# Chunk 0 of a hybrid decoder block's MLP as seven block products, with the block sums of chunks 0 to 2 formed by transfers

## The chip, the cores and the metric

The kernel runs on one core of one Trainium2 chip. The metric is the device time of one execution in microseconds (us); a kernel's time is the median of several executions. TensorE (PE; PEld is its weight load), VectorE (DVE), ScalarE (ACT), GpSimd (POOL) and SyncE (SP) each run their own instructions in order and wait for one another through semaphores.

## The reference

One layer of a causal decoder on 256 tokens of width 1024, all in float32: a convolution branch and a sparse attention branch from one input projection, a cross attention over 256 memory tokens, and a squared-ReLU MLP. The change lies in the MLP:

```python
hf = _rmsnorm(h, norm_ffn_g[l]) @ w_ff1[l]             # 1024 -> 4096
h = h + jnp.square(jax.nn.relu(hf)) @ w_ff2[l]         # 4096 -> 1024
...
return _rmsnorm(h, norm_final_g)
```

## The kernel before

*Numbers.* Matrix products are made in float32r from operands split in two: `hi` is the rounded value (a Copy on ScalarE), `lo` the rest (a subtraction on VectorE). A product a @ b is three matmuls, a_hi b_hi + a_hi b_lo + a_lo b_hi (`mm3`). With activations held as hi and lo side by side, an f1 tile can be "wide": eight matmuls of 512 columns and eight of 256 in place of 24 narrow ones of 256. A wide tile leaves two halves that must be merged (a Copy on ScalarE, line 444, and an add on VectorE); a narrow one goes straight into the Relu (line 1208).

*The weight stream.* All weights come in 1 MB chunks through transfers issued on SP's queue (`fetch`, line 178), into three rotating `raws` buffers, and for some chunks into `t8` buffers. `high_jobs` lists what is to be split next; `split_high` issues one ScalarE copy (line 295 in `high`, line 273 in `seven`) if a slot is free (six `highs`/`lows`, less those held), and `split_low` issues the VectorE subtraction of the copy before. `split_ahead` calls both, and a step of TensorE's work calls it once or so. A chunk's buffer is handed back by `release`, which issues the next load. The order of all engines' instructions is thus written out by the program; nothing is moved by a scheduler.

*The chains.* Work that follows a product (activations, norms, the 16 small transfers that turn `h_t` into `h_rm`, line 1200) is written as generators. Each `tick` advances every running generator by one `yield`, and so places its next instructions into the engines' queues at that point.

*The MLP.* f1 and f2 are cut into 16 chunks of 256 hidden features. `first` makes chunk c + 2's f1 tiles (two of 128 features), and `half_of` adds chunk c's part to the output, half before and half after the second f1 tile. Tokens are two row blocks of 128, and f2's chunk is a 2 x 2 block matrix (128 x 512 each). Chunks 1 to 13 (`SEVEN`) use a seven-product scheme: four stages `left`, `last`, `outer` and `inner` with 2, 1, 2 and 2 block products, which need sums of f2's blocks (`sums`) and differences of the activations' blocks (`t[:, 4:8]` in `activation`). VectorE forms the four sums of a chunk with one add of 128x1024 and two of 128x512 (`outer` and `inner` in `seven`). ScalarE's copies of the sums read them directly. Chunk 0 is instead made with eight products (`half_of`, `c not in SEVEN`), and its activation goes by halves (`by_halves`); chunk 2's f1 tiles, made beside chunk 0, are wide, those of the later chunks narrow (`wide` in the loop). f1 of chunks 0 and 1 comes before the loop, through `form_b_late` and `form_b`.

*Banks.* The seven partial sums stay open in PSUM over all chunks: "2", "3", "4", "5" in the four `ps_acc` banks, "7" in one of the two `ps_mm` banks, "1" and "6" in the two `ps_aux`. f1's tiles of the loop use what is left of `ps_mm`.

*POOL.* GpSimd issues 25 adding transfers for the convolution (line 628, `accum_op=ALU.add`, 256 KB each) up to 172 us, a few small operations, and one memset of `table` near the end of the program (line 1423). Line 81 is the helper through which all TensorE and VectorE instructions are recorded.

Of the kernel before, what the change touches and what calls it, by code (L numbers as in the profile page):

```python
# [8 lines left out]
F32 = mybir.dt.float32  # L9
# [3 lines left out]
ALU = mybir.AluOpType  # L13
# [3 lines left out]
P = 128  # L17
D = 1024
S = 256
KT = D // P  # L20
# [33 lines left out]
INDEX = {c: n for n, c in enumerate(c for c in STREAM if c[0] != "ki")}  # L54
# [2 lines left out]
HALVES = 6  # L57
EARLY = (3,)
WHOLE = (("conv", 0),)
SEVEN = tuple(range(1, 14))  # L60
JOINED = 14
FIRST = STREAM.index(("f1", 2))
BY_HALVES = ()

# [51 lines left out]
def block_kernel(ctx, tc, x, xt, mem, memt, wst, wki, vecs, convw, gout, out):  # L116
# [15 lines left out]
    def t8(name, dt=F32, shape=(P, KT, S)):  # L132
        return big.tile(list(shape), dt, tag="t8", bufs=12, name=name)
# [16 lines left out]
    def ps_acc(name):  # L150
        return bank("acc", 4, name)
# [12 lines left out]
    prepared, whole, elsewhere = {}, {}, set()  # L164
    order = [c for c, key in enumerate(STREAM) if key[0] != "f1" or key[1] < 3]
    early = set(EARLY)
    raw_of, landed = {}, set()
    high_jobs, low_jobs = [], []

    def fetch(c, raw, parts=1, only=None):  # L170

        key = STREAM[c]
        n = KT * NK if key[0] == "ki" else N_CHUNK
        src = wki if key[0] == "ki" else wst[INDEX[key]]
        for q in range(parts):
            if only in (None, q):
                ns = slice(q * n // parts, (q + 1) * n // parts)
                nc.sync.dma_start(raw[:, ns], src[:, ns])
        raw_of[c] = raw
        landed.update((key, q) for q in ((0, 1) if only is None else (only,)))  # L180
# [61 lines left out]
    def seven(key, c):  # L242

        def b():
            return raw_of[c].rearrange("p (k h n) -> p k h n", k=2, h=2)

        def flat():
            return raw_of[c].rearrange("p (j n) -> p j n", j=4)

        sums = []  # L250

        def outer():
            sums.append(t8(f"sums{c}", F32, (P, 4, 512)))
            dve.tensor_tensor(out=sums[0][:, 0:2, :], in0=flat()[:, 0:4:3, :],
                              in1=flat()[:, 1:2, :].to_broadcast([P, 2, 512]), op=ALU.add)

        def inner(j):
            t = sums[0]
            dve.tensor_tensor(out=t[:, j, :], in0=t[:, j - 1, :], in1=flat()[:, 2 * j - 4, :], op=ALU.add)
            if j == 3:  # L260
                release(key, c, 1, True)

        def stage(name, src_of, n, steps=()):
            def high():
                src = src_of()
                if steps:
                    both = t8(f"{name}{c}", F32R, (P, 2, 2, 512))
                    hi, lo = both[:, 0], both[:, 1]
                else:
                    hi = highs.tile([P, N_CHUNK // 2], F32R, tag="hi", name=f"hi{c}{name}")  # L270
                    lo = lows.tile([P, N_CHUNK // 2], F32R, tag="lo", name=f"lo{c}{name}")
                    hi, lo = (w[:, : n * 512].rearrange("p (j n) -> p j n", j=n) for w in (hi, lo))
                act(hi, src, AF.Copy)  # L273

                def low():
                    dve.tensor_tensor(out=lo, in0=src, in1=hi.bitcast(F32), op=ALU.subtract)
                    prepared[(*key, name)] = (hi, lo)

                low_jobs.append(low)

            return Stage((*key, name), high, steps, not steps, (key, 0))

        return [stage("left", lambda: b()[:, :, 0, :], 2), stage("last", lambda: flat()[:, 3:4, :], 1),
                stage("outer", lambda: sums[0][:, 0:2, :], 2, (outer,)),
                stage("inner", lambda: sums[0][:, 2:4, :], 2, (lambda: inner(2), lambda: inner(3)))]

# [35 lines left out]
    def weights(kind, i, half, kt):  # L322

        key = (kind, i, half)
        while key not in prepared:
            split_high()
            split_low()
        nused[0] += key not in elsewhere
        return [w if kt is None else w.rearrange("p (k n) -> p k n", k=kt) for w in prepared.pop(key)]
# [18 lines left out]
    def split_ahead():  # L348
        split_low()
        split_high()  # L350

    def tick():
        for c in list(chains):
            if next(c, "end") == "end":
                chains.remove(c)
        while (len(fill) > 1 or (fill and (len(done) > 5 or nused[0] < 5))) and dve.total < pe.total - 1000:
            fill_one()
        dve.total = max(dve.total, pe.total - 2000)
        add_some()
# [30 lines left out]
    def tile_b(ps, w, x2, kts=range(KT), wide=False, late=False):  # L390


        ps = ps[: w[0].shape[2]]
        for kt in kts:
            wh, wl = w[0][:, kt, :], w[1][:, kt, :]
            if not wide:
                mm_b(ps[:, :S], wh, wl, x2, kt, kt == 0, kt == KT - 1)
            elif kt == 0:
                pe.matmul(ps, wh, x2.both(kt), start=True, stop=False)
                if late:  # L400
                    pe.matmul(ps[:, S:], wl, x2.high(kt), start=False, stop=False)
            elif not late:
                pe.matmul(ps, wh, x2.both(kt), start=False, stop=False)
            else:
                pe.matmul(ps[:, S:], wl, x2.high(kt), start=False, stop=False)
                pe.matmul(ps, wh, x2.both(kt), start=False, stop=kt == KT - 1)
        for kt in kts if wide and not late else ():
            pe.matmul(ps[:, S:], w[1][:, kt, :], x2.high(kt), start=False, stop=kt == KT - 1)
# [5 lines left out]
    def form_b(kind, i, x2, after, ps_of=ps_mm):  # L414

        for ct in range(2):
            w = weights(kind, i, ct, KT)
            split_ahead()
            ps = ps_of(f"ps_{kind}{i}{ct}")
            wide = is_wide(kind, 2 * i + ct)  # L420
            tile_b(ps, w, x2, wide=wide)
            after(2 * i + ct, ps if wide else ps[:, :S])
            tick()
# [753 lines left out]
    for hf in range(2):  # L1177
        nc.sync.dma_start(g_out[hf], gout[hf * 512 : hf * 512 + 512].partition_broadcast(P))
    fetch(STREAM.index(("f1", 3)), t8("raw_f1", F32, (P, N_CHUNK)))
    r2 = []  # L1180

    def ff_scale():
# [31 lines left out]
    def part(c, t, js, sh, sl):  # L1214
        act(sh[:, js, :], t, AF.Copy)
        yield
        dve.tensor_tensor(out=sl[:, js, :], in0=t, in1=sh[:, js, :].bitcast(F32), op=ALU.subtract)

    def by_halves(c, ct, ps, t, sh, sl):
        js = slice(2 * ct, 2 * ct + 2)  # L1220
        yield from relu(ps, t[:, js, :].rearrange("p r n -> p (r n)"))
        act(t[:, js, :], t[:, js, :], AF.Square)
        yield
        yield from part(c, t[:, js, :], js, sh, sl)
        if c == 0 and ct:
            dve.tensor_tensor(out=t[:, 4:6, :], in0=t[:, 1:4:2, :], in1=t[:, 0:4:2, :], op=ALU.subtract)
            yield
            yield from part(c, t[:, 4:6, :], slice(4, 6), sh, sl)

    def activation(c, ct, ps, t, sh, sl):  # L1230
        if c in (0, 15):
            yield from by_halves(c, ct, ps, t, sh, sl)
            return
        yield from relu(ps, t[:, 2 * ct : 2 * ct + 2, :].rearrange("p r n -> p (r n)"))
        if ct == 0:
            return
        act(t[:, 0:4, :], t[:, 0:4, :], AF.Square)
        yield
        js = slice(0, 4)
        if c in SEVEN:  # L1240

            dve.tensor_tensor(out=t[:, 4:6, :], in0=t[:, 0:1, :].to_broadcast([P, 2, P]), in1=t[:, 1:3, :], op=ALU.subtract)
            yield
            dve.tensor_tensor(out=t[:, 6, :], in0=t[:, 1, :], in1=t[:, 5, :], op=ALU.subtract)
            yield
            dve.tensor_tensor(out=t[:, 7, :], in0=t[:, 3, :], in1=t[:, 6, :], op=ALU.subtract)
            yield
            js = slice(1, 8)
        elif c < JOINED:
            dve.tensor_tensor(out=t[:, 4:6, :], in0=t[:, 1:4:2, :], in1=t[:, 0:4:2, :], op=ALU.subtract)  # L1250
            yield
            js = slice(0, 6)
        yield from part(c, t[:, js, :], slice(0, js.stop - js.start), sh, sl)
# [21 lines left out]

    hidden = [Hidden(0), Hidden(1)]
    form_b_late("f1", 0, f2, hidden[0].after, ps_of=ps_acc)
    form_b("f1", 1, f2, hidden[1].after, ps_acc)

    uses = {}  # L1280
    for c in range(JOINED):
# [35 lines left out]
    def first(x, side, wide):  # L1317
        ps = ps_mm(f"ps_f{x.c}{side}")
        w = weights("f1", x.c, side, KT)
        split_ahead()  # L1320
        tile_b(ps, w, f2, wide=wide)
        x.after(side, ps if wide else ps[:, :S])
        tick()
        if wide:
            tick()
# [188 lines left out]
```

## Time and profile before

| | us |
|---|---|
| median of 3 runs (501.36 to 501.70) | 501.44 |
| the profiled execution | 501.41 |
| its span, first to last instruction | 499.6 |
| TensorE busy | 490.8 (98%) |
| VectorE busy | 465.5 (93%) |
| ScalarE busy | 349.0 (70%) |
| GpSimd busy | 30.6 (6%) |

The profiled execution's time lies 0.03 us under the median, so its rows can be set against the runs as they are. Times in rows are us from the span's start. The MLP begins at about 322.6 (the first f1 matmul) and the last f2 matmul ends at 488.3. Line 81 appears for nearly all TensorE and VectorE rows, so these are told apart by the tiles they write and read (`ps_f` for f1, `ps_p` for f2's products, `fs` and `ft` for activations, `sums`, `outer`, `inner` for the seven scheme). Instructions overlap their neighbours by some 0.09 us on VectorE, so the sum of durations is a little over the time taken.

### The profile page before, as it was taken

Reading aid. Unit: us, or ns where it says so; the run is one execution under the profiler, and the core shown is the slowest. Engines: PE = TensorE matmul, PEld = TensorE weight load, DVE = VectorE, ACT = ScalarE, POOL = GpSimd, SP = SyncE. Lnnn points to the kernel's source line nnn. Section 1 sums busy time; section 2 is a strip of 40 time slices with the busy share of each in tenths; the row PEclk is TensorE's granted clock in tenths of the full one; section 3 lists DMA queues with packets and bytes.
Section 4 is the critical chain, followed back from the end, with each engine's and each line's share of the span. In section 5 each row is a group of like instructions: output and inputs, shape, how many; then the busy total and the mean of one; then the engine's idle time right before and its main releaser. Section 6 shows DMA issues by size and latency. Waiting matters only on the chain.

```text
span 499.6 us, 8287 instructions
## 1 busy us (share of the span) xinstructions
PE 490.8 (98%) x3120; PEld 444.3 (89%) x3120; DVE 465.5 (93%) x847; ACT 349.0 (70%) x606; POOL 30.6 (6%) x47
## 2 busy tenths in 40 slices
PE   7999999999999999999999999999999999999995
PEld 6999998888888889888889999988999999999984
DVE  5999899999999789999988997799999999999996
ACT  7657777788756666767846567687777667777752
POOL 2002212221111100000000000000000000000000
PEclk9999999999999999999999999999999999999999
DMA  8959688899887653444655553765666456655412
GB/s 317 378 190 280 174 195 264 238 243 279 240 219 224 180 178 104 152 169 173 249 169 183 220 188 110 269 186 132 195 234 222 171 185 213 234 208 173 131 81 84
DMA packets 28376, 100.35 MB, mean 201 GB/s; under 512 B 10784, under 2 KB 11552, under 8 KB 19376
## 3 DMA queue, kind: packets, MB, share of 16 engines
q1 hardware_dynamic: 24416, 93.03, 54.7%
q0 software_dynamic: 3632, 6.59, 7.4%
q8 instruction: 24, 0.39, 0.3%
q10 hardware_dynamic: 288, 0.20, 0.1%
q14 instruction: 16, 0.13, 0.1%
HBM read 91.16 MB, written 1.05 MB: 185 GB/s over the span
## 4 chain that ended last, share of the span: by engine, by line
PE 92%; DVE 5%; DMA 1%; ACT 1%; issue 1%; POOL 0%; DVEq 0%; SPq 0%; ACTq 0%; POOLq 0%
PE ps_f L81 18%; PE ps_p L81 15%; PE ps_conv L81 10%; PE ps_co L81 5%; PE ps_ao L81 4%; PE ps_ga L81 4%; PE ps_gc L81 4%; PE ps_q L81 4%; PE ps_k L81 4%; PE ps_v L81 4%; PE ps_xo L81 3%; PE ps_qi L81 2%; PE ps_xk L81 2%; PE ps_xv L81 2%; PE ps_xq L81 2%; PE ps_mix L81 1%
## 5 line engine op out<-in xcount | busy, mean ns | idle before, releaser
L81 DVE TENSOR_TENSOR lo<-raw,hi 128x1024 fp32r<-128x1024 f32 x133 | 161.2, 1215 | 3.3 <-ACT hi L295 3.0
L295 ACT ACTIVATE hi<-raw 128x1024 fp32r<-128x1024 f32 x133 | 138.5, 1046 | 0.9 <-DMA raw<-in_wst_dram 0.9
L81 PE MATMUL ps_f<-ff_p,hi 128*128 128x256 f32 (+1 forms) x464 | 89.2, 294 | 0.0
L81 PEld LDWEIGHTS ps_f<-ff_p,hi 128*128 128x128 f32 x464 | 75.3, 191 | 3.7
L81 DVE SCALAR_TENSOR_TENSOR acc<-u,cw,acc 128x234 f32<-128x234 f32 (+29 forms) x190 | 78.1, 463 | 0.3
L81 PE MATMUL ps_f<-ff_p,lo 128*128 128x256 f32 x256 | 67.5, 283 | 0.0
L81 PEld LDWEIGHTS ps_f<-ff_p,lo 128*128 128x128 f32 x256 | 47.2, 191 | 0.4
L81 PE MATMUL ps_conv<-n_p,hi 128*128 128x256 f32 x224 | 41.0, 285 | 0.0
L81 PEld LDWEIGHTS ps_conv<-n_p,hi 128*128 128x128 f32 x224 | 34.9, 192 | 0.8 <-issue 0.7
L81 PE MATMUL ps_conv<-n_p,lo 128*128 128x256 f32 x112 | 31.7, 283 | 0.0
L628 POOL DMA_DIRECT2D acc<-products x25 | 21.7, 867 | 125.6 <-ACT products L627 53.1
L273 ACT ACTIVATE inner<-sums 128x1024 fp32r<-128x1024 f32 x13 | 13.8, 1061 | 20.6 <-DVE sums L81 20.6
L627 ACT ACTIVATE products<-u,cw 128x231 f32<-128x231 f32 (+24 forms) x50 | 21.9, 488 | 0.0
L81 PEld LDWEIGHTS ps_conv<-n_p,lo 128*128 128x128 f32 x112 | 21.5, 192 | 0.0
L1208 ACT ACTIVATE ft<-ps_f 128x256 f32<-128x256 f32 x26 | 9.9, 380 | 14.7 <-PE ps_f L81 14.7
L81 PE MATMUL ps_p<-outer,fs 128*128 128x512 f32 x78 | 20.1, 393 | 0.0
L81 PE MATMUL ps_v<-hi,n_p 128*128 128x512 f32 x64 | 19.9, 389 | 0.0
L81 PE MATMUL ps_p<-inner,fs 128*128 128x512 f32 x78 | 19.8, 389 | 0.0
L81 PE MATMUL ps_co<-u_p,hi 128*128 128x512 f32 (+1 forms) x80 | 19.3, 350 | 0.0
L81 PE MATMUL ps_mix<-mix_p,hi 128*128 128x512 f32 (+1 forms) x80 | 19.2, 349 | 0.0
L81 DVE TENSOR_TENSOR sums<-sums,raw 128x512 f32<-128x512 f32 x26 | 17.8, 684 | 0.0
L81 PEld LDWEIGHTS ps_p<-inner,fs 128*128 128x128 f32 x78 | 14.6, 188 | 3.0
(424 smaller groups left out, 1168.0 us busy)
## 6 DMA issues: line engine op xcount, KB each, us to landing
raw<-in_wst_dram SPq DMA_DIRECT2D x67, 1024.0 KB, 5.5
raw<-in_wst_dram SPq DMA_DIRECT2D x28, 512.0 KB, 4.4
acc<-products POOLq DMA_DIRECT2D x25, 256.0 KB, 6.4
x_rm<-in_x_dram SPq DMA_DIRECT2D x2, 512.0 KB, 4.0
mem_rm<-in_mem_dram SPq DMA_DIRECT2D x1, 1024.0 KB, 9.1
mem_t<-in_memt_dram SPq DMA_DIRECT2D x1, 1024.0 KB, 11.1
h_t<-in_xt_dram SPq DMA_DIRECT2D x1, 1024.0 KB, 6.9
raw_f<-in_wst_dram SPq DMA_DIRECT2D x1, 1024.0 KB, 9.5
```

The lines of the kernel that those rows point to most:

```text
L81: return fn(*args, **kwargs)
L273: act(hi, src, AF.Copy)
L295: act(hi, raw[:, ns], AF.Copy)
L627: act(prod[:, a, s:], u[:, t, : S - s], AF.Copy, scale=cw[:, t, TAPS - 1 - s : TAPS - s])
L628: nc.gpsimd.dma_start(acc[:, ts, :], prod, accum_op=ALU.add)
L1208: act(t, ps, AF.Relu)
```

## The change

Chunk 0 joins `SEVEN`. For chunks 0, 1 and 2 (`ADDED`) the block sums are no longer made by VectorE. Right after the load of f1's chunk 3 is issued, POOL issues for each of them two plain transfers of 512 KB from the weights in HBM into a `sums` tile, then an adding one of 512 KB (its second block, read twice), an adding one within SBUF of 512 KB (`sums[1]`, read twice), and an adding one of 256 KB; chunks 0 and 1 go side by side, chunk 2 after them. Chunk 0's `outer` and `inner` use `highs`/`lows` slots instead of `t8` buffers. In the activations of chunks 0 to 2 two `yield`s between the small subtractions are dropped. f1's tiles of chunk 1 get two ticks ahead of `after` and one behind it, and chunk 2's tiles one more.

```diff
-SEVEN = tuple(range(1, 14))
+SEVEN = tuple(range(14))
 JOINED = 14
+ADDED = (0, 1, 2)
...
         def outer():
+            if added:
+                sums.append(added_sums[key[1]])
+                return
             sums.append(t8(f"sums{c}", F32, (P, 4, 512)))
             dve.tensor_tensor(out=sums[0][:, 0:2, :], ...)
         def inner(j):
             t = sums[0]
-            dve.tensor_tensor(out=t[:, j, :], in0=t[:, j - 1, :], in1=flat()[:, 2 * j - 4, :], op=ALU.add)
+            if not added:
+                dve.tensor_tensor(out=t[:, j, :], in0=t[:, j - 1, :], in1=flat()[:, 2 * j - 4, :], op=ALU.add)
             if j == 3:
                 release(key, c, 1, True)
...
-                if steps:
+                if steps and key[1] > 0:
                     both = t8(f"{name}{c}", F32R, (P, 2, 2, 512))
...
-            return Stage((*key, name), high, steps, not steps, (key, 0))
+            return Stage((*key, name), high, steps, not steps or key[1] == 0, (key, 0))
...
     fetch(STREAM.index(("f1", 3)), t8("raw_f1", F32, (P, N_CHUNK)))
+    for group in ((0, 1), (2,)):
+        for c in group:
+            added_sums[c] = t8(f"sums{c}", F32, (P, 4, 512))
+        blocks = {c: wst[INDEX[("f2", c)]].rearrange("p (j n) -> p j n", j=4) for c in group}
+        for c in group:
+            nc.gpsimd.dma_start(added_sums[c][:, 0:2, :], blocks[c][:, 0:4:3, :])
+            nc.gpsimd.dma_start(added_sums[c][:, 2:4, :], blocks[c][:, 0:4:2, :])
+        for c in group:
+            nc.gpsimd.dma_start(added_sums[c][:, 0:2, :], blocks[c][:, 1:2, :].to_broadcast([P, 2, 512]), accum_op=ALU.add)
+        for c in group:
+            nc.gpsimd.dma_start(added_sums[c][:, 2:4, :], added_sums[c][:, 1:2, :].to_broadcast([P, 2, 512]), accum_op=ALU.add)
+        for c in group:
+            nc.gpsimd.dma_start(added_sums[c][:, 3, :], blocks[c][:, 0, :], accum_op=ALU.add)
...
-        if c == 0 and ct:
-            dve.tensor_tensor(out=t[:, 4:6, :], in0=t[:, 1:4:2, :], in1=t[:, 0:4:2, :], op=ALU.subtract)
-            yield
-            yield from part(c, t[:, 4:6, :], slice(4, 6), sh, sl)
     def activation(c, ct, ps, t, sh, sl):
-        if c in (0, 15):
+        if c == 15:
             yield from by_halves(c, ct, ps, t, sh, sl)
...
             dve.tensor_tensor(out=t[:, 4:6, :], in0=t[:, 0:1, :].to_broadcast([P, 2, P]), in1=t[:, 1:3, :], op=ALU.subtract)
-            yield
+            if c > 2:
+                yield
             dve.tensor_tensor(out=t[:, 6, :], in0=t[:, 1, :], in1=t[:, 5, :], op=ALU.subtract)
-            yield
+            if c > 2:
+                yield
             dve.tensor_tensor(out=t[:, 7, :], in0=t[:, 3, :], in1=t[:, 6, :], op=ALU.subtract)
...
     form_b_late("f1", 0, f2, hidden[0].after, ps_of=ps_acc)
-    form_b("f1", 1, f2, hidden[1].after, ps_acc)
+    for side in range(2):
+        w = weights("f1", 1, side, KT)
+        split_ahead()
+        ps = ps_acc(f"ps_f11{side}")
+        tile_b(ps, w, f2, wide=True)
+        tick()
+        tick()
+        hidden[1].after(side, ps)
+        tick()
...
         tile_b(ps, w, f2, wide=wide)
+        if x.c == 2:
+            tick()
         x.after(side, ps if wide else ps[:, :S])
         tick()
```

`first` is called with `wide = c not in SEVEN and c != 5` for chunk c + 2, so with chunk 0 in `SEVEN` no f1 tile of the loop is wide.

More of the change, by code (lines that the diff above doesn't have):

```diff
@@ L166, in block_kernel @@
     early = set(EARLY)
-    raw_of, landed = {}, set()
+    raw_of, landed, added_sums = {}, set(), {}
     high_jobs, low_jobs = [], []
@@ L248, in flat @@
             return raw_of[c].rearrange("p (j n) -> p j n", j=4)
-        sums = []
+        sums, added = [], key[1] in ADDED
         def outer():
+            if added:
+                sums.append(added_sums[key[1]])
+                return
             sums.append(t8(f"sums{c}", F32, (P, 4, 512)))
```

## The prediction

> **What bounds the kernel now.** I read the engine shares first, then the chain that ended last, then its pieces in order of time around the MLP's first chunks, where the edits lie.
>
> ```profile
> span 499.6 us, 8287 instructions
> PE 490.8 (98%) x3120; PEld 444.3 (89%) x3120; DVE 465.5 (93%) x847; ACT 349.0 (70%) x606; POOL 30.6 (6%) x47
> PE 92%; DVE 5%; DMA 1%; ACT 1%; issue 1%; POOL 0%; DVEq 0%; SPq 0%; ACTq 0%; POOLq 0%
> ```
>
> TensorE carries 92% of the chain, so an edit pays only where it shortens TensorE's own work or closes one of its gaps. The pieces (start, length, what):
>
> ```profile
> 292.19 3.74 PE ps_xq L81 x29
> ...
> 306.54 1.13 PE ps_xs L81 x4
> ...
> 322.64 13.97 PE ps_f L81 x80
> 336.61 0.34 PE ps_ff L81 x4
> 336.95 3.09 PE ps_p L81 x12
> 340.04 2.77 PE ps_f L81 x16
> 342.81 2.75 PE ps_p L81 x12
> 345.56 2.87 PE ps_f L81 x24
> 348.43 2.07 PE ps_p L81 x9
> 350.50 2.87 PE ps_f L81 x24
> 353.37 2.75 PE ps_p L81 x12
> 356.12 2.87 PE ps_f L81 x24
> 358.99 2.07 PE ps_p L81 x9
> 361.06 2.87 PE ps_f L81 x24
> ```
>
> From 322.64 every piece begins where the last one ends: five wide f1 tiles (13.97 / 5 = 2.79 each), the four small matmuls of the row norms, chunk 0 as 24 matmuls (3.09 + 2.75) around a wide tile of chunk 2 (2.77), then chunk 1 with narrow tiles (2.87) and 9 + 12 matmuls (2.07 + 2.75). Twelve matmuls that wait for nothing take 2.75; chunk 0's first twelve take 3.09. The 0.34 between is the one gap, and the waits name it (total, times, longest):
>
> ```profile
> PEld ps_p L81 <- ACT fs L1215: 0.3, 1, 0.3
> PEld ps_p L81 <- DVE fs L81: 0.2, 1, 0.2
> ```
>
> That is chunk 0's activation, finished too late for its first products. VectorE has no reserve in this stage, but ends early enough (third row: columns PE, PEld, DVE, ACT busy, DMA share next to last):
>
> ```profile
> 38.00:172.00 134.00, 134.00 (x841) 120.01 (x840) 129.71 (x285) 98.04 (x183) 25.47 (x29) 1.00 0.83 235
> 297.00:322.00 25.00, 24.90 (x187) 23.80 (x186) 18.48 (x39) 16.91 (x38) 0.35 (x2) 1.00 0.57 200
> 337.00:359.00 22.00, 22.00 (x134) 19.44 (x134) 21.34 (x32) 15.79 (x24) 0.00 (x0) 1.00 0.64 161
> ```
>
> **The change part by part.** *Chunk 0 as seven products.* 24 matmuls become 21, in the 9 + 12 of chunk 1: 2.07 + 2.75 = 4.82 in place of 3.09 + 2.75 = 5.84. Of the 1.02 saved, 0.68 is three matmuls and 0.34 the gap, if it closes. Chunk 0 in SEVEN also makes both f1 tiles of chunk 2 narrow: 2 x (2.87 - 2.77) = +0.20. Sum on TensorE: -0.82.
>
> *Chunk 0's activation and the ticks.* Its chain grows (one Square over both halves, three small subtractions, one copy and one subtraction of 896 columns), so does the gap close? The edit gives the f1 tiles of chunk 1 three ticks each instead of one, and drops two yields, so the chain's steps stand earlier in every queue. I laid the queues out by hand from the rows of before: VectorE frees up at 328.7, then one 1.22 split, three 0.69 and 0.42 adds for the norm's sums, the merge of the second half (0.42), the three subtractions (0.42, 0.28, 0.28), the split of "left" (1.22), a merge, the norm's two scalars, and chunk 0's last subtraction (1.08) come to 336.5, each start being some 0.09 before the end of the one ahead.
>
> ```profile
> L81 DVE TENSOR_TENSOR fs<-ft,fs 128x896 fp32r<-128x896 f32 x13 | 14.1, 1083 | 0.0
> L81 DVE TENSOR_TENSOR ft<-ft 128x128 f32<-128x128 f32 x26 | 7.4, 284 | 0.0
> 338.37 0.42 DVE L81 TENSOR_TENSOR fs<-ft,fs 128x256 fp32r<-128x256 f32 x1
> ```
>
> The first product would be ready to start at 322.64 + 4 x 2.79 + 0.34 + 2.87 = 337.0, so the operand is there 0.5 early, where it ended at 338.8 before. Bounds: nothing to +0.8, the latter if every margin of 0.5 that I find for chunk 0 (also "outer" and the f1 half of chunk 3) is missed by a little. I take zero.
>
> *The norm's four small matmuls* move ahead of chunk 2's first tile, because of the ticks. They need the folded sums, by my layout at 332.5, and TensorE reaches them at 333.8. Cost zero, bound 0.3. The transfers of h_rm, one a tick, also go out some four ticks earlier on SP's queue, 0.63 each, ahead of loads that may so start up to 2.5 late.
>
> *Block sums off VectorE.* Chunks 1 and 2 lose one 128x1024 and two 128x512 adds each.
>
> ```profile
> L81 DVE TENSOR_TENSOR sums<-raw 128x1024 f32<-128x1024 f32 x13 | 15.8, 1218 | 0.0
> L81 DVE TENSOR_TENSOR sums<-sums,raw 128x512 f32<-128x512 f32 x26 | 17.8, 684 | 0.0
> ACT inner L273 <- DVE sums L81: 20.6, 12, 2.7
> ```
>
> That is 1.22 + 2 x 0.68 = 2.59 per chunk, and chunk 0's seven form would otherwise have cost the same. The time is worth nothing by itself, since TensorE does not wait for VectorE after 340; it is what makes room for chunk 0's extra splits (left, last, outer, inner: 1.22 + 0.68 + 1.22 + 1.22 against the two of 1.22 before).
>
> *The transfers on POOL's queue.* Per chunk two plain 512 KB transfers, two adding 512 KB and one adding 256 KB, fifteen in all. POOL is free early, and the one thing queued behind them, the clearing of `table` at 317.44, is read only by the last norm, at the end.
>
> ```profile
> 296.55 0.70 POOL L501 TENSOR_TENSOR rs_cx<-ms_cx,half 128x2 f32<-128x2 f32 x1 [64.48 <-DVE ms_cx L81]
> 317.44 0.10 POOL L1423 MEMSET table<- 128x1 f32 x1 [20.19 <-ACT table L1130]
> L628 POOL DMA_DIRECT2D acc<-products x25: 852/862/908, 38.9 to 172.4; - x25
> DMA to landing us min/median/max: 3.3/6.4/8.9
> q1 hardware_dynamic: 24416, 93.03, 54.7%
> q0 software_dynamic: 3632, 6.59, 7.4%
> ```
>
> The buffers are no hindrance: sums 0 and 1 take those of mix_p, whose last matmul is ahead of the piece at 292.19, and sums 2 that of qx, last read by the piece at 306.54. So the first group starts at 297.3. The price of one adding transfer is in the trace: 25 of 256 KB from POOL's queue (the convolution taps) landed after 3.3 to 8.9 us, median 6.4. For size I use the queues' shares: q0 took 0.074 x 499.6 / 6.59 = 5.6 us per MB of all 16 engines, q1 0.547 x 499.6 / 93.03 = 2.9. So 512 KB adding is 6.4 + 1.5 = 7.9, and 512 KB plain 6.5 (1.5 of transfer in either case). Sums 2 wait for seven landings one behind another, since POOL issues in order and waits for chunk 1's second adds before it comes to the second group: plain 299.0 to 305.5; adds of chunk 1, behind chunk 0's on the same ring (+1.5), to 314.9 and 324.3; issue of the last add; plain to 331.7; adds to 339.6, 347.5 and, 256 KB, 353.9. With every landing at its shortest it is 332, with every one at its longest 371. Sums 0 are whole four landings after 297.3, by some 328, sums 1 by 332.
>
> When are they needed? ScalarE copies inner of chunk 0 at about 339.5 by my layout, of chunk 1 at 348. For chunk 2 the trace shows how late the copy may be:
>
> ```profile
> 359.18 1.06 ACT L273 ACTIVATE inner<-sums 128x1024 fp32r<-128x1024 f32 x1 [2.70 <-DVE sums L81]
> 360.15 0.37 ACT L1208 ACTIVATE ft<-ps_f 128x256 f32<-128x256 f32 x1
> ```
>
> Behind it in ScalarE's order stands the Relu that empties the bank of chunk 4's first f1 tile. The product "7" holds one of the two ps_mm banks, so the next f1 tile (361.06) waits for that Relu, which ended at 360.52: 0.54 to spare. The copy may thus start at 359.18 + 0.54, less the 0.82 that TensorE is ahead: 358.9. My 353.9 leaves 5 us. That is a cover and not a certainty: each us beyond 358.9 is a us of TensorE.
>
> A rule speaks against this. The Trainium skill (SBUF — State Buffer, "SBUF: two separate sides") says that transfers issued from GpSimd starve while VectorE runs in a two-port mode, because their descriptors can't be written. The 25 landings above carry whatever of that there is: VectorE was busy 129.71 of 134.00 us there, at a DMA share of 0.83, as against 18.48 of 25.00 at 0.57 and 21.34 of 22.00 at 0.64 where the new transfers run. So the median may be used here, and it is more likely long than short.
>
> *The loads on SP's queue* share the engines with 7.1 MB more (15 transfers).
>
> ```profile
> 314.78 0.33 SPq L178 DMA_DIRECT2D raw<-in_wst_dram  x1
> 328.99 1.06 ACT L295 ACTIVATE hi<-raw 128x1024 fp32r<-128x1024 f32 x1
> raw<-in_wst_dram SPq DMA_DIRECT2D x67, 1024.0 KB, 5.5
> ```
>
> Chunk 0's f2 block is asked for at 314.78, lands some 5.5 later and is read at 328.99: 8.7 in hand, which covers a doubled transfer and the SP delay above. Cost zero, bound 2. The releases of f2 0 to 2 no longer wait for VectorE's sums and come sooner.
>
> *Sum.* -0.68 - 0.34 + 0.20 = -0.82 on an execution of 501.41 (span 499.6 and 1.8 around it), 0.03 below the median 501.44: 500.6.
>
> **The rivals.** *Sums 2 land late* (the slower side). Seven draws between 3.3 and 8.9, put at a deviation of 1.6 each, make 4.2 about 353.9, so 358.9 is passed about once in eight, and I add for things unlike the taps: 2 KB rows out of HBM, a repeated source, two transfers in one ring. It decides from 358.9 on; from 360.7 it is slower than before by over 0.2%, at the longest landings (371) 12 us: 513. A middling case, 362, is 503.7.
>
> *Chunk 0 comes late by small waits.* VectorE's order has margins of 0.5 to 0.7 at four places; if the gap stays (0.34) and half a us is added, nothing is won: 501.4. For it: the chain is longer than the one that was late. Against it: its steps stand sooner in every queue.
>
> *The change is hidden anyway, or the transfers slow all else.* If ScalarE meets unfinished sums 0, or loads are late by over 8 us, several us are lost at once: 504. Against it: 11 us in hand.
>
> *The skill's rule at full force*: each of the seven at its longest, the 513 of the first rival; it is in that chance.
>
> **How the numbers follow.** Forecast (no new wait worth naming, -0.8 within 0.3): 0.66. Late sums 2: 0.18. Small waits: 0.12. Everything late: 0.04. A difference of 0.2%, 1.0 us, is about what a measurement of this kernel can tell. The forecast lies just inside it, so of its 0.66 I give 0.16 to more than 1.0 faster; the small waits and a fifth of the late case stay within. Faster 0.16, same 0.65, slower 0.19. The forecast's own range is 500.3 to 501.1. The range reaches up to a middling late case and leaves out the worst: 500.2 to 502.8.
>
> **What would show it.** ps_p pieces of 2.07 and 2.75 for chunk 0 and no wait of PEld for fs; ps_f of 2.87 for chunk 2; six fewer rows of sums on VectorE (chunks 1 and 2); "ACT inner <- DVE sums" replaced for chunks 0 to 2 by no wait, or by "<- DMA sums", which is the rival; sums 2 landing before 358.9. I am wrong if POOL's transfers start much after 297.3, land slower than 9 us each, or if TensorE shows a gap in 337 to 365.

## The result and the profile after

The changed kernel takes 505.27 us (median of 7 runs, 504.84 to 509.43), the kernel before 501.70 in the same session (7 runs): a ratio of 1.0096, 95% interval 1.008 to 1.0112. The forecast was 500.6 and its range ended at 502.8, so it was wrong. The first rival (sums 2 land late) came true, at more than its price. The profiled execution took 505.08 against 501.41 before: 3.67 us to account for.

The first lines of the page after:

```profile
span 503.3 us, 8334 instructions
PE 491.9 (98%) x3133; PEld 445.7 (89%) x3133; DVE 463.6 (92%) x841; ACT 350.0 (70%) x603; POOL 44.8 (9%) x62
PE 68%; issue 17%; DMA 10%; DVE 3%; ACT 1%; POOL 1%; DVEq 0%; SPq 0%; POOLq 0%
```

TensorE's busy time rose by 1.1 us, with fewer matmuls in the products. The chain now runs through transfers (DMA 10%), and those stretches lie ahead of one place. In the pieces of the chain in order of time (start, length):

```profile
353.59 4.73 DMA sums<-in_wst_dram
358.32 3.15 issue
361.47 1.06 ACT inner L278
362.53 0.28 ACT ft L1226
362.81 0.04 issue
362.85 4.27 PE ps_f L82 x24
367.12 3.14 PE ps_p L82 x12
370.26 2.87 PE ps_f L82 x24
```

The last adding transfer of sums 2 is issued at 353.59; ScalarE copies the sums at 361.47; the Relu behind that copy empties a bank at 362.8, and chunk 4's second f1 tile starts there. It then takes 4.27, where such a tile takes 2.87 without a wait and 3.13 behind one (the zero matmuls below), and the products behind it take 3.14 in place of 2.75. What ScalarE was kept by and what it did next (timeline), and how long the transfer issued at 353.59 took to land (its own line, 7.8 us to 361.4; the 4.73 of the chain is that of its packets):

```profile
DMA to landing us min/median/max: 7.8/7.8/7.8
361.47 1.06 ACT L278 ACTIVATE inner<-sums 128x1024 fp32r<-128x1024 f32 x1 [5.59 <-issue]
362.85 0.50 PE L82 MATMUL ps_f<-ff_p,hi 128*128 128x256 f32 x2 [2.29 <-ACT ft L1226]
```

The copy's row names no releaser ("issue"); that it waited for the transfer follows from the landing at 361.4, and in a later kernel the row of its wait names it. Why that tile takes 4.27 is in the granted clock of the windows (the third column from the right):

```profile
360.00:362.00 2.00, 0.56 (x3) 0.14 (x1) 0.00 (x0) 0.53 (x1) 0.00 (x0) 1.00 1.08 363
362.00:364.00 2.00, 1.15 (x9) 1.15 (x10) 1.29 (x2) 1.96 (x4) 0.00 (x0) 1.00 1.04 424
364.00:366.00 2.00, 2.00 (x13) 2.00 (x12) 2.00 (x2) 2.00 (x3) 0.00 (x0) 0.60 0.71 295
366.00:368.00 2.00, 2.00 (x9) 1.79 (x8) 2.00 (x3) 1.02 (x3) 0.00 (x0) 0.55 0.73 229
368.00:370.00 2.00, 2.00 (x10) 1.63 (x9) 2.00 (x5) 2.00 (x3) 0.00 (x0) 1.00 0.08 33
```

The clock falls to half at about 364.4, a us and a half after TensorE has gone back to work, and stays there for some 3.4 us. That costs 4.27 - 3.13 = 1.14 on the tile and 0.39 on the products, 1.53 us in all.

The account goes by rows of the timeline before and after. (A piece of the chain begins where the one ahead ends, its row some 0.16 earlier, so pieces and rows can't be mixed.) Chunk 3's first f1 tile, before and then after:

```profile
345.40 0.40 PE L81 MATMUL ps_f<-ff_p,hi 128*128 128x256 f32 x2
344.73 0.40 PE L82 MATMUL ps_f<-ff_p,hi 128*128 128x256 f32 x2
```

It starts 0.67 ahead, where 0.82 was forecast. A small wait takes 0.17 back. Chunk 4's second f1 tile, due at 360.40, starts at 362.85, 2.45 late. Its first matmuls behind the pause take 0.10 longer, and the half clock costs 1.53. -0.67 + 0.17 + 2.45 + 0.10 + 1.53 = 3.58, which is how the next tile stands (pieces 370.26 against 366.68), and 0.09 comes later.

Where the chain lost its time is in POOL's own rows (chunk 1's transfers of each kind, then all of chunk 2's):

```profile
298.73 0.72 POOL L1190 DMA_DIRECT2D sums<-in_wst_dram  x1
...
306.79 1.21 POOL L1193 DMA_DIRECT2D sums<-in_wst_dram  x1 [2.33 <-DMA sums<-in_wst_dram]
...
316.16 1.20 POOL L1195 DMA_DIRECT2D sums<-sums  x1 [2.63 <-DMA sums<-in_wst_dram]
...
326.52 0.85 POOL L1197 DMA_DIRECT2D sums<-in_wst_dram  x1 [4.69 <-DMA sums<-sums]
327.08 1.04 POOL L1190 DMA_DIRECT2D sums<-in_wst_dram  x1
...
336.66 1.22 POOL L1193 DMA_DIRECT2D sums<-in_wst_dram  x1 [7.91 <-DMA sums<-in_wst_dram]
344.38 1.23 POOL L1195 DMA_DIRECT2D sums<-sums  x1 [6.49 <-DMA sums<-in_wst_dram]
353.59 0.91 POOL L1197 DMA_DIRECT2D sums<-in_wst_dram  x1 [7.99 <-DMA sums<-sums]
```

From 298.73 to 361.4 are 62.7 us, where the prediction had 54.9: the steps are 8.1, 9.4, 10.4, 0.6, 9.6, 7.7, 9.2 and 7.8, where it had 6.5, 9.4, 9.4, 0.9, 6.5, 7.9, 7.9 and 6.4. And the load under which they ran, in windows (DMA share next to last; before, then after):

```profile
337.00:360.00 23.00, 23.00 (x139) 20.23 (x139) 22.34 (x34) 16.61 (x25) 0.00 (x0) 1.00 0.63 158
337.00:360.00 23.00, 23.00 (x148) 20.73 (x147) 19.94 (x27) 16.77 (x23) 3.13 (x4) 1.00 1.06 218
```

### The profile page after: what moved, and what is told of

The parts are those of the page before. It is cut to its first block, busy times and chain, and to the rows that moved or that the text cites. A ratio compares the mean times of both kernels' runs of the same rounds, so it can differ in the third digit from the quotient of the medians.

```text
span 503.3 us, 8334 instructions
## 1 busy us (share of the span) xinstructions
PE 491.9 (98%) x3133; PEld 445.7 (89%) x3133; DVE 463.6 (92%) x841; ACT 350.0 (70%) x603; POOL 44.8 (9%) x62
## 3 DMA queue, kind: packets, MB, share of 16 engines
HBM read 96.67 MB, written 1.05 MB: 194 GB/s over the span
## 4 chain that ended last, share of the span: by engine, by line
PE 68%; issue 17%; DMA 10%; DVE 3%; ACT 1%; POOL 1%; DVEq 0%; SPq 0%; POOLq 0%
PE ps_f L82 13%; PE ps_p L82 12%; PE ps_conv L82 10%; DMA sums<-in_wst_dram 7%; PE ps_ga L82 4%; PE ps_gc L82 4%; PE ps_q L82 4%; PE ps_k L82 4%; PE ps_v L82 4%; PE ps_qi L82 2%; PE ps_xk L82 2%; PE ps_xv L82 2%; DMA sums<-sums 2%; PE ps_s L82 1%; PE ps_o L82 1%
## 5 line engine op out<-in xcount | busy, mean ns | idle before, releaser
L82 DVE TENSOR_TENSOR lo<-raw,hi 128x1024 fp32r<-128x1024 f32 x131 | 158.6, 1214 | 4.3 <-ACT hi L300 3.2
L300 ACT ACTIVATE hi<-raw 128x1024 fp32r<-128x1024 f32 x131 | 136.4, 1047 | 0.8 <-DMA raw<-in_wst_dram 0.7
L82 PE MATMUL ps_f<-ff_p,hi 128*128 128x256 f32 (+1 forms) x480 | 92.4, 293 | 2.3 <-ACT ft L1226 2.3
L82 PEld LDWEIGHTS ps_f<-ff_p,hi 128*128 128x128 f32 x480 | 78.0, 193 | 6.1 <-ACT ft L1226 3.0
L82 PE MATMUL ps_f<-ff_p,lo 128*128 128x256 f32 x256 | 70.3, 285 | 0.0
L82 PEld LDWEIGHTS ps_f<-ff_p,lo 128*128 128x128 f32 x256 | 48.6, 193 | 0.3
L82 DVE TENSOR_TENSOR inner<-sums,inner 128x1024 fp32r<-128x1024 f32 x13 | 15.8, 1216 | 4.2 <-ACT inner L278 4.2
```

The lines of the kernel that those rows point to most:

```text
L82: return fn(*args, **kwargs)
L300: act(hi, raw[:, ns], AF.Copy)
```

## The experiments

The theory: sums 2 come late, at the end of seven landings, and each us of it stops TensorE; the pause then costs the clock. The rivals: the bytes crowd the loads of weights, and the wait on sums 2 only marks it; or chunk 0 as seven products costs too. Medians stand against the kernel before in the same session (501.46 to 501.72).

**Chunk 2's sums by VectorE again.** `ADDED = (0, 1)`, one group of ten transfers.

> Chunk 2's sums go back to VectorE, five of the fifteen transfers are gone, all else is as after the change. Theory (the last landing of sums 2 holds ScalarE, and through the Relu and the one free ps_mm bank TensorE): no gap at chunk 4's second f1 tile, TensorE's clock stays full, 500.7 (500.3 to 501.1), 0.8 under before. Rival A (7 MB of extra transfers slow loads and everything else): only a third of the loss comes back, 503.5 to 504.5. Rival B (chunk 0's seven-product form, its chain or the ticks cost the time): 504.5 to 505.5, as after the change.

501.29 us, ratio 0.999 (0.9982 to 0.9999): all of the loss is gone. Less than forecast is won: two f1 tiles wait for a Relu and take 3.07 and 3.11 for 2.87. The first does so in the changed kernel too; the second stands behind ScalarE's copy of the sums that VectorE makes again. In its pieces chunk 3's first f1 tile starts 0.64 ahead of before (344.92 against 345.56), the two waits take 0.20 and 0.24 back, and -0.20 is left; the profiled executions differ by 0.10 (501.31 against 501.41). The medians differ by 0.43, more than the traces account for.

```profile
349.86 3.07 PE ps_f L82 x24
...
360.62 3.11 PE ps_f L82 x24
```

**The fifteen transfers interleaved**, chunk 2's between those of chunks 0 and 1:

```diff
-    for group in ((0, 1), (2,)): ...
+    for step, c in ((plain, 0), (plain, 1), (add1, 0), (add1, 1), (plain, 2), (add2, 0), (add2, 1), (add1, 2),
+                    (add3, 0), (add3, 1), (add2, 2), (add3, 2)):
+        step(c)
```

> The same fifteen transfers with the same bytes, issued in another order on POOL: chunk 2's plain ones go right behind the first adds of chunks 0 and 1, its first add behind their second adds, so that four landings and not seven lie ahead of its last add. Theory: sums 2 are whole at about 345 in place of 361.4, ScalarE's copy of inner 2 waits for nothing, 500.7 (500.3 to 501.1). Rival A (extra bytes): still 503 to 505, since every byte still moves. Rival B (chunk 0 itself): 505.

505.25, ratio 1.0069 (1.005 to 1.0088): a miss. Sums 2 are whole at 347.39 + 9.1 = 356.5, later than the 345 that I expected but in time, and other things are late. Two of its waits, and a row of SP's queue, where eight of the transfers that turn h take 16.52 us to issue (8 x 0.67 before):

```profile
ACT hi58left L278 <- DMA raw<-in_wst_dram: 4.3, 1, 4.3
ACT hi L300 <- DMA raw<-in_wst_dram: 2.9, 1, 2.9
330.69 16.52 SPq L1225 DMA_DIRECT2D h_rm<-turned  x8
```

Loads of weights stand behind these on SP's queue. So sums 2 are not the only thing that the transfers can make late, and the first rival is not ruled out.

**No transfers at all.** `ADDED = ()`: VectorE sums for all chunks, chunk 0 still as seven products.

> No transfers on POOL: chunk 0 as seven products and the ticks as after the change, but VectorE forms the sums of chunks 0, 1 and 2 (7.8 us more of VectorE between 329 and 360, 2.6 of them in chunk 0, where its margin was 0.5). Theory: the transfers were needed for chunk 0: its outer or inner stage comes 1 to 3 us late, a gap on TensorE near 342, 501.5 to 504.5. Rival (VectorE has room enough, the transfers bought nothing): 500.6.

506.18, ratio 1.0107 (1.0071 to 1.0144), worse than I had thought. TensorE now waits in many places:

```profile
PEld ps_f L82 <- ACT ft L1226: 3.0, 2, 1.6
PE ps_f L82 <- ACT ft L1226: 2.1, 2, 1.2
```

In this order of the queues chunk 0 in seven products pays only with some of the sums taken off VectorE: with those of chunks 0 and 1 off it, the time was 501.29.

**The clock by itself.** Ten matmuls with weights of zero, into an open bank, ahead of chunk 4's second f1 tile, so that TensorE has no pause:

```diff
+        if (x.c, side) == (4, 1):
+            for n in range(10):
+                nc.tensor.matmul(banks["1"], nought, f2.both(n % KT), start=False, stop=False)
```

> As after the change, with ten matmuls of 512 columns and a weight of zeros into the open bank 1, put ahead of chunk 4's second f1 tile, where TensorE stood for 2.3 us: 2.3 us of work that adds nothing to the result. Theory on the clock (the half clock from 364.4 to 368.5 followed from the idle time, and cost some 1.8 us beside the gap): with TensorE kept busy the clock stays at 1.00 and the run is about 1.8 us shorter than after the change, 503.3 where sums 2 land as in its profile. Rival (the clock fell for another reason, or the ten matmuls only add their time): 505 to 507.5.

The profiled execution took 503.67, with the sums copied as late as ever (361.70), and the clock at 1.00 in every window from 358 to 384. Its pieces:

```profile
361.70 1.06 ACT inner L278
...
363.08 3.13 PE ps_f L82 x24
366.22 2.75 PE ps_p L82 x12
```

By rows, -0.67 + 0.17 + 2.68 late + 0.10 on the first matmuls = 2.28, and 503.67 - 501.41 = 2.26. From the copy's start to chunk 5's first f1 tile it takes 7.10 us, and 8.63 in the changed kernel: the half clock is a cost of its own, 1.53 us (the 1.8 expected has the tile's restart in it), and follows from the pause. The median of the five runs is 504.83 (503.67 to 514.4), which by itself does not tell theory from rival; the one trace does.

**One landing more.** One extra plain transfer of chunk 2's first two sums, ahead of its first adding one.

> Dose. Chunk 2's chain gets one more plain transfer of its first two sums, which the adding transfer then waits for: one more serial landing of 8 to 9.5 us; nothing else changes. Theory (sums 2 are the late thing, and each us of their lateness is a us of TensorE): sums 2 whole at about 370 instead of 361.4, TensorE idle before chunk 4's second f1 tile for 10 to 12 us instead of 2.6, time 505.3 + 8 to 9.5 = 513 to 515 (a little less if a longer pause costs no more clock than the short one did). Rival (the loads crowd each other, and the wait on sums 2 merely marks it): the added transfer is one in sixteen and the time rises by 1 us or less, to 506.

Its two runs took 512.76 and 517.87 (ratio 1.0264, 1.0196 to 1.0333). In the profiled one the copy starts at 369.2 (the piece after the landing), 7.7 later, and the execution is 7.7 longer, us for us. The longest wait of a weight load is now 10.4 us, and the tile behind it and its products cost about what they cost after the short pause (4.61 and 2.75, which is 1.48 over 3.13 and 2.75):

```profile
PEld ps_f L82 <- ACT ft L1228: 10.8, 2, 10.4
370.57 4.61 PE ps_f L82 x24
375.18 2.75 PE ps_p L82 x12
```

So in these two traces lateness costs its own length, and the half clock about 1.5 us more, for a pause of 2.3 as for one of 10.

**Chunk 2's transfers with a quarter of the columns.** The other columns of its sums are left at zero.

> Chunk 2's five transfers carry only the first 128 of the 512 columns of each block (the other columns of its sums are set to zero by GpSimd, so chunk 2's products are not the reference's); their number and order stay. Theory (lateness of sums 2 is all of the loss): with a quarter of the bytes the five landings take 4 to 6 us each instead of 8 to 9.6, sums 2 are whole at 343 to 353, ahead of the 358.9 at which ScalarE wants them, TensorE does not stop, and the prediction's own sum holds: 501.7 - 0.82 = 500.9, between 500.6 and 501.2. If a landing is a fixed time and not bytes, sums 2 stay at about 360 and the time at 504 to 505. Rival (something else of the change costs too): sums 2 in time and the time still over 502.

501.15 (12 runs, 500.96 to 508.19; before 501.51; ratio 1.0001, 0.9972 to 1.003), the profiled one 501.08. The five transfers land sooner, but by far less than the bytes (plain 5.7 in place of 10.1, adds 4.0, 7.0 and 5.7 in place of 7.2, 8.9 and 7.8, each from its own row), and start 5.4 later (chunk 1's last add is issued 4.1 later, and the clearing of the rest comes between); sums 2 are whole at 350.72 + 5.7 = 356.4, later than I expected and in time:

```profile
332.48 1.07 POOL L1194 DMA_DIRECT2D sums<-in_wst_dram  x1
...
350.72 0.91 POOL L1201 DMA_DIRECT2D sums<-in_wst_dram  x1 [6.10 <-DMA sums<-sums]
```

With sums 2 in time the rest of the change costs TensorE nothing in this trace but the 0.19 of one small wait (chunk 3's second f1 tile, 3.06 for 2.87). But chunk 2's bytes, too, are a quarter here, so the kernel does not show what the full load does to the loads of weights.

**One landing less in each group.** The third adding transfer right behind the first, on which it does not depend, so that five landings and not seven lie one behind another ahead of whole sums 2:

```diff
         for c in group:
             (first adding transfer, block 1 onto sums 0 and 1)
+            nc.gpsimd.dma_start(added_sums[c][:, 3, :], blocks[c][:, 0, :], accum_op=ALU.add)
```

> The third adding transfer of each chunk (block 0 onto the fourth sum) is issued right behind the first one, on which it does not depend, and the second adding transfer, sums onto sums, comes last: same fifteen transfers, same bytes, one serial landing less in each group. Theory (length of the chain): group of chunks 0 and 1 ends some 8 us earlier, chunk 2's chain is another landing shorter, so sums 2 are whole at 345 to 352 instead of 361.4; no stop of TensorE, 500.7 to 501.3. Rival (the load of the DMA engines sets the landings, not the number of steps): the same bytes in less time land later each, loads of weights and chunk 0's sums come late as in the interleaved order, and the time stays at 503 to 505.

504.37, ratio 1.0051 (1.0021 to 1.0082): better than the change by about a us, but still slower than before. Sums 2 are whole at 345.94 + 9.2 = 355.1, later than expected and in time. The two landings saved were partly paid back, since the landings beside one another grew (chunk 2's plain ones to 12 to 13). What is late is a load of weights. Pieces of its chain, then SP's row:

```profile
355.87 1.94 SPq L1217
357.91 5.98 DMA raw<-in_wst_dram
363.91 1.07 ACT hi L300
330.78 12.08 SPq L1217 DMA_DIRECT2D h_rm<-turned  x8
```

The loads behind the last turning transfer are issued from 357.91 on, 3.3 later than in the changed kernel (354.62); the first takes 5.98 to land, and ScalarE's half of its split was already due (it waited 4.6 us, VectorE's half 5.0). Here loads of weights are late while sums 2 are in time: the rival's mechanism, without the theory's.

**The turning transfers later.** The 16 transfers from `turned` to `h_rm` held back until chunk 4:

```diff
+                while not turn_now:
+                    yield
                 nc.sync.dma_start(rows[32 * b : 32 * b + 32, :, a, :], ...)
...
+        if c == 4:
+            turn_now.append(1)
```

> The sixteen transfers that turn the rows of h (h_rm from turned) are held back until chunk 4's products, that is about from 385 on, instead of 334 to 358; all else as in the changed kernel. Theory with the load as the cause of the long landings: without them the DMA engines' share falls from 1.08 to about 0.9 between 334 and 358, landings fall from 8 to 9.6 us to 6.5 to 8, sums 2 are whole at 352 to 358, and the time is 500.9 to 501.5. If the landings are set by the adding transfers themselves, sums 2 stay at 360 to 361.4 and the time at 504 to 505.3. Rival: the held transfers slow the loads of weights behind them on SP's queue later on, and waits on raw tiles appear after 385: over 502 whatever sums 2 do.

507.49 (12 runs from 500.88 to 513.85; ratio 1.0084, 1.005 to 1.0117), which neither theory gave. Two runs are at 500.88 and 501.25, most at 507.3 to 507.9. In the profiled one (513.85) TensorE pauses for 4.0 us ahead of 201, before any instruction that the change touches, and all that follows comes 6.9 later. A second trace was to be free of that pause:

> The changed kernel with the turning transfers held back, a second time, for a trace without the pause that its first one had long before the change (TensorE stopped between 180 and 205 us there, and everything behind it came some 7 us later). Theory (both latenesses count, and this edit takes away only that of the loads): no wait on a raw tile, but sums 2 still come at the end of seven landings: where they are whole by 359 the time is 500.9 to 501.3, where they come at 361 to 363 TensorE pauses, loses 2 to 4 us and the half clock of about 1.8 us, and the time is 504.5 to 507.5; the trace shows which of the two it was, with the chain of chunk 2 at 30 to 32 us from its first issue to its last landing instead of 34.3. Rival (the times of 507 belong to the loads behind the turning transfers in 385 to 425): waits on raw tiles there.

506.72 (4 runs, 504.99 to 508.17; ratio 1.0111, 1.0094 to 1.0129). Its trace (504.99) has no wait on a raw tile worth naming, the DMA share between 337 and 360 is 0.80 in place of 1.06, and sums 2 are late all the same: chunk 2's chain takes 30.6 us (330.80 to 361.40) where it took 34.3, but starts 3.7 later.

```profile
330.80 1.04 POOL L1190 DMA_DIRECT2D sums<-in_wst_dram  x1
...
356.10 5.30 DMA sums<-in_wst_dram
ACT inner L278 <- DMA sums<-in_wst_dram: 5.5, 1, 5.5
```

So the lighter load did shorten chunk 2's own landings. The first trace says the same: 30.1 us there at a share of 0.86, against 34.3 both in the changed kernel and with the zero matmuls (1.06 and 1.05). But the group of chunks 0 and 1, which ends about when the first held transfer would have gone out, took 32.0 us from 298.80, and 28.4 from 298.73 in the changed kernel. It was as slow in the kernel with a quarter of the columns, whose first group is the same (its last adding transfer is issued at 330.60, at 326.52 in the changed kernel). Why the first group differs so from trace to trace is not shown; it ate up what the lighter load gave, and the seven landings end at 361.4 again. Two landings fewer brought sums 2 in 6 us earlier. Why most runs of the first session were at 507 no trace shows.

**Both edits, one landing less and the turning transfers later.**

> The two edits together: the third adding transfer right behind the first one (one serial landing less), and the sixteen turning transfers of h held back to chunk 4's products. Theory, in its second form (two things are late because of the crowding at 330 to 358: sums 2 at the end of seven landings, and the loads of weights that stand on SP's queue behind turning transfers, eight of which took 11.46 us to issue in the changed kernel and 12.08 with the one landing less): with both gone no tile of TensorE waits for a copy of sums or of a raw load; sums 2 whole at 345 to 353; TensorE's own sum of -0.82 with 0.2 of waits back: 500.9 to 501.2. Rival (the bytes of the fifteen transfers themselves are too much for the DMA engines): loads stay late without the turning transfers, 503 to 505.

501.15 (11 runs, 500.85 to 507.02; before 501.50; ratio 0.9993, 0.9965 to 1.002), the profiled one 500.85. Sums 2 are whole at 355.3, a little later than expected, the copy waits for nothing, and SP issues fourteen loads in the time in which it was held by turning transfers:

```profile
326.73 52.03 SPq L179 DMA_DIRECT2D raw<-in_wst_dram  x14
355.76 1.04 ACT L278 ACTIVATE inner<-sums 128x1024 fp32r<-128x1024 f32 x1
```

Each edit alone leaves one of the two latenesses, and both together leave none.

**The interleaved order with the turning transfers later.**

> The interleaved order of the fifteen transfers again (505.25 before), now with the turning transfers of h held back to chunk 4's products. Theory (in the interleaved order SP's queue was the loss: eight turning transfers took 16.52 us to issue, and the loads behind them came late): the loads issue when their buffers come free, no wait on raw tiles, 501 to 502, the rest being chunk 0's sums, which land at about 340. Rival (the order itself is the loss, chunk 0's sums late and the engines full): 504 or more.

501.33 (10 runs; ratio 0.9996, 0.9987 to 1.0005), from 505.25. So the interleaved order had lost most of its time to the turning transfers. The edit takes away both their place on SP's queue and their load, and the runs don't part the two. What is left is chunk 0's sums, which land at 341.29 and hold up a split and a Relu (waits of 0.4 and 0.8 on TensorE):

```profile
328.24 13.05 DMA sums<-in_wst_dram
345.50 3.14 PE ps_f L82 x24
```

**A Relu ahead of a copy**, on top of both edits, for the small wait: `split_ahead` called behind the tile in chunk 3's first f1 tile.

> As the kernel with one landing less and the turning transfers held back, and in chunk 3's first f1 tile the Relu of the tile goes ahead of ScalarE's copy of chunk 1's first sums (one pair of instructions changes places). Theory: the 0.19 us by which chunk 3's second f1 tile waits for that Relu (its piece 3.06 in place of 2.87) goes, and nothing else: 0.2 us under that kernel, 500.7 to 501.0. Rival: the copy of the sums, 0.4 us later, makes its products late instead and the time is equal or 0.2 higher.

501.72 (11 runs; ratio 0.9999, 0.9983 to 1.0016), 0.6 worse than without and more than the rival allowed. The wait on the Relu is gone, and another took its place: `split_ahead` also places VectorE's half of a weight split, which moved back with it.

```profile
PEld ps_f L82 <- DVE lo L82: 0.9, 1, 0.9
```

No version beats the kernel before by more than 0.1%. Of those below it, chunk 2's sums back on VectorE is the steadiest (501.21 to 501.56 in 12 runs).

## Why the prediction was wrong

*What held.* TensorE's own sum in the main: -0.82 forecast, -0.67 measured at chunk 3's first f1 tile, and an execution 0.56 shorter where one small wait is all that is left (500.85). The difference lies ahead of chunk 0's products: their first row is at 337.04 where by the forecast it would be some 0.2 earlier, in part since chunk 2's first tile, behind the norm's matmuls, takes 2.98 (2.87 forecast; piece of the kernel with chunk 2's sums on VectorE). The layout of the queues held too: the operand of chunk 0's first products at 336.5 (its subtraction starts at 335.44), the norm's matmuls (row at 333.72, 333.8 forecast), POOL's start at 297.2 (297.3), and the wait for sums 2 as the place where it would break. The deadline: the tile was due at 360.40 and starts 1.38 behind the copy, so the copy had until 359.0; 358.9 was forecast.

*The step that failed* is the price of a landing. I took 6.5 for a plain transfer of 512 KB, 7.9 for an adding one and 6.4 for 256 KB; chunk 2's took 10.1, 7.2, 8.9 and 7.8 (lines of each). The largest part is the plain transfers: the steps from their issue to the first adding transfer are 8.1 and 9.6 in place of 6.5, 4.7 of the 7.5 us by which sums 2 came behind 353.9. All 25 landings of before were of adding transfers of 256 KB, so no row of theirs gave the 6.5. The adding steps were off by -0.2 to +1.4. The taps' landings came from a stage at a share of 0.83, and I argued that the new transfers would run at 0.64, the share before them. But with them it was 1.06. I had put the change's own load on the loads of weights and not on its own chain. That the load counts is shown by chunk 2's chain, 34.3 us at that share and 30 to 31 at 0.80 to 0.86; it had 28.7 in the forecast. How the rest divides between the load, the size and what else is on the queue is not shown. Nor was it a bad draw: the chain of seven landings took 62.6 to 63.6 us in all four traces that have it. I had taken seven independent draws about the taps' landings, with a spread of 4.2, where the middle itself was too low, and 0.18 was too little for that rival.

*The term that was missing* is the clock. The rival said "each us beyond 358.9 is a us of TensorE". By that rule a copy at 361.47 gives 501.41 - 0.82 + 2.6 = 503.2. Measured were 505.08; 1.5 of the 1.9 us more are the half clock, the rest small waits and TensorE's smaller gain.

*The cost put at zero that was not, though hidden:* the loads on SP's queue. I counted the turning transfers at 0.63 each. In the changed kernel eight took 11.46 us to issue. No wait on a load shows there, since ScalarE stood for sums 2 in any case. With those in time it depended on when the loads behind the last turning transfers went out: from 357.91, with one landing less, they were late; from 353.64, with a quarter of the columns, they kept ScalarE for 0.4 us and TensorE not at all.

*The rule of the Trainium skill* that I weighed (SBUF — State Buffer, "SBUF: two separate sides": transfers from GpSimd starve under VectorE's two-port mode) is not shown by these runs. VectorE was less busy in 337 to 360 than before (19.94 us against 22.34) while landings grew. No run here varies VectorE's mode alone.

## What to carry to other kernels

A chain of transfers is priced step by step at the load that it makes itself; what is taken off it gives back less than its share (three quarters of chunk 2's bytes, three tenths of its chain's time; two landings of 8 to 9 us, 6). When a margin of 5 us stands on seven durations from another stage, look first for what they have in common: an error in their middle adds up seven times. And before holding two causes against each other, take away both: here either edit alone left 3 to 6 us of loss, and both together left none.

## What the runs showed of the hardware

*The clock.* A pause of TensorE of 2.3 us between matmuls (2.7 between weight loads) was followed by half clock for some 3.4 us, which began 1.5 us after work had resumed. In the interleaved order a pause of 2.0 us ahead of 358.62 was enough (window of 359 to 361, granted clock third from the right):

```profile
359.00:361.00 2.00, 2.00 (x12) 2.00 (x11) 1.76 (x4) 2.00 (x3) 0.00 (x0) 0.51 0.78 299
```

The Trainium skill (TensorE: Matmul & The Clock Gate, "Why this matters for your kernels") warns of pauses of over about 3 us; here shorter ones sufficed, and the measurement decides. Pauses of up to 1.4 us, in the kernel with one landing less, left the clock at 1.00.

*Landings.* The Trainium skill (DMA: Bandwidth & Descriptors, "Anatomy of one DMA — SWDGE (gpsimd) path") fits one transfer from GpSimd by 2.0 us and the bytes at 436 GB/s, which is an estimated 3.2 us for 512 KB. No landing of that size was under 5.2 us in these runs, where the engines' share was mostly near 1, and in the interleaved order with the turning transfers later one took 19.0. So the estimate was passed by 2 us at the least, and the traces decide.

*Issuing.* SP's issue of a turning transfer (64 KB within SBUF) took 0.67 us before (2.68 for 4), 1.43 in the changed kernel (11.46 for 8) and 2.07 in the interleaved order (16.52 for 8). The engines' share between 337 and 345 was 0.71, 1.11 and 1.18 in these three: issues were slower where the share was higher, and the loads behind them on the queue went out later (from 354.62 in the changed kernel, from 357.91 where eight took 12.08).
